# A mixture-of-experts decoder block: down-projection rows loaded in pairs, up-projection columns taken in the matching order, and the overflow table moved into the expert loop

## The chip, the cores and the metric

The kernel runs on one core of a Trainium2 chip. The metric is the device time of one execution in microseconds (us); several executions are timed and their median is given. Beside them one execution is taken with the hardware profiler, and every row below is from that one. TensorE multiplies matrices (its results go to PSUM), VectorE and ScalarE do the elementwise work, GpSimd issues the scattered writes, and SyncE's queue (SP) issues the weight loads, which 16 DMA engines carry out.

## The reference

One decoder block on 512 tokens of width 1024, all in float32: adaLN-modulated RMS norms, a gated linear recurrence (HGRN2) beside sliding-window attention, a merge, and then a mixture of 32 experts of which each token takes 4. The change is in the last part:

```
logits = h @ w_router + b_router;  gates = softmax(top 4 of logits)
per expert e, on the tokens that chose it:
    hu    = x @ w_up[e] + b_up[e]                 # 1024 -> 2048
    x_glu = min(hu[:, ::2], 7);  x_lin = clip(hu[:, 1::2], -7, 7)
    act   = x_glu * sigmoid(1.702 * x_glu) * (x_lin + 1)
    y     = act @ w_down[e] + b_down[e]           # 1024 -> 1024
out = x + g2 * sum over a token's experts of gate * y
```

Even columns of `w_up` make the gated half and odd columns the linear half.

## The kernel before, in words

Matrices are multiplied in fp16 with three products: each float32 weight tile of 128 partitions by 2048 floats is split into a high part (ScalarE, L341: `hi = fp16(w*2048)`) and a low part (VectorE, L346: `lo = fp16(w*2048 - hi)`), and TensorE adds hi*hi, hi*lo and lo*hi. The function `split` does this for all stages. It takes a loaded tile from a ring of 8 KB-per-partition buffers (named slot, slotb, slotc) and a second buffer of the same ring for the two fp16 halves. A staging buffer comes free when the low part is made, a split buffer when the matmuls that read it are done, and with each buffer that comes free `pump` issues the next load of a fixed list on SP's queue.

Each expert has 8 up tiles (128 rows of `w_up`, 2048 columns: one run of 8192 bytes per partition) and 4 down tiles (256 rows of `w_down`: two rows of 4096 bytes per partition, 128 rows apart). The first 3 down tiles are split, the last one goes to TensorE as float32. In the up split the even and odd columns are parted: `view_in` reads the tile as "all even columns, then all odd columns", a step of 2 floats within a partition, and the halves are written without a step. So row p of hidden block f of `act` is the hidden unit 128 f + p, which is what the down tile has in partition p.

The loop over experts is software-pipelined: for expert e come 8 steps of `up_k` (48 matmuls each), with the gather of the next expert's tokens between them (`pick`, L1150, copied by ScalarE at L1157), then `swiglu` (L1199 to L1216, VectorE and ScalarE in turn), then the down projection of expert e-1 (`down_j`), and its output rows scaled by `finish` (L1253) and added to DRAM by an indirect DMA (L1245). `up_bias` (L1183) puts the bias into the up banks. Splits run ahead of the matmuls: `ahead(i)` makes all splits up to LOOK = 6 tiles past tile i. Ahead of `swiglu` a further call, with `lows`, makes the high part of one more tile at once and its low part only after `swiglu`.

An expert's 96 token slots can overflow. `overflow_table` works out on VectorE how many further blocks there are, and a loop of that many trips runs after all experts; with these inputs it made none. The table is computed in the last trip of the expert loop, before the last down projection. The instructions of each engine run in the order in which the program issues them (L1388 to L1396 fix it).

L635 and the reductions L506, L993 and L1282, which the prediction uses as measures, are elsewhere: L635 multiplies columns 2s-1, 4s-1, ... of a tile by columns s-1, 3s-1, ... in place, for s = 1, 2, 4, ..., with 512/s elements a partition; L993 sums over 4 runs that lie 32 floats apart; L506 and L1282 sum over contiguous runs. L851 and L960 are plain multiplications and additions without a step, L1004 a plain ScalarE copy.

Of the kernel before, what the change touches and what calls it, by code (L numbers as in the profile page):

```python
# [41 lines left out]
def block_body(tc, x, c, positions, w_ada, b_ada, norm1_gain, w_in, lower_bound_logits, hg_norm_gain,  # L42
# [19 lines left out]
    with top:  # L62
# [41 lines left out]
        def dview(ap, off, dims):  # L104
            return bass.AP(tensor=ap.tensor, offset=ap.offset + off, ap=dims)
# [55 lines left out]
        def q_dn(e, j):  # L161
            queue(("dn", e, j), lambda t: SP.dma_start(
                t.rearrange("p (k f) -> p k f", k=2),
                dview(w_down, (e * 1024 + 256 * j) * 1024, [[1024, 128], [128 * 1024, 2], [1, 1024]])))
# [876 lines left out]
        def bias_up():  # L1041
            st = ready.pop(("bup",))
            src = st[:32, :].rearrange("p (f g) -> p g f", g=2)
            bk = sd_bank()
            for m in range(16):
                T.transpose(bk[:, 32 * m:32 * m + 32], src[:, m // 8, 128 * (m % 8):128 * (m % 8) + 128],
                            ident[:32, :32])
            A.activation(bu.rearrange("p e m -> p m e"), bk.rearrange("p (m e) -> p m e", m=16), AF.Copy, scale=SU)
            free(st)
# [7 lines left out]
        def split_up(e, k, later=None):  # L1057
            split(("up", e, k), 2048, later=later, view_in=lambda t: t.rearrange("p (f g) -> p g f", g=2),
                  view_hi=lambda t: t.rearrange("p (g f) -> p g f", g=2))
# [126 lines left out]
        def up_k(hl, k, xg):  # L1186
            for f in range(16):
                o = pu[f // 4][:, C * (f % 4):C * (f % 4) + C]
                for n, (pa_, pw) in enumerate(PASSES):
                    T.matmul(o, lhsT=hl[:, 2048 * pw + 128 * f:2048 * pw + 128 * f + 128], rhs=xg[:, pa_, k, :],  # L1190
                             start=False, stop=(k == KT - 1 and n == 2), skip_group_check=True)
# [65 lines left out]

        def overflow_table():
# [17 lines left out]
            V.tensor_copy(nblk[:, 0:1], cum[:, NE - 1:NE])  # L1276
            slot = hl_take()[0]
# [4 lines left out]
            V.tensor_reduce(eix, cmpt, axis=AX.X, op=OP.add)  # L1282
            eixi = moe.tile([128, NB], I32, name="eixi")
# [4 lines left out]
            V.tensor_sub(cum, cum, nbk)  # L1288
            V.tensor_tensor(cmpt, iota_e[:, None, :].to_broadcast([128, NB, NE]),
# [6 lines left out]
            return nblk, eix, eixi, beg  # L1296
# [39 lines left out]

        i = 0
        for e in range(NEX + 1):
            if e < NEX:
                prep = nexts.pop(e + 1, iter(()))  # L1340
                xg = state[e][0]
                for k in range(8):
# [4 lines left out]
                    hl_done(("up", e, k))  # L1347
                    i += 1
# [8 lines left out]
                ahead(i, lows)  # L1357
# [9 lines left out]
            if e == NEX:  # L1367
                tables = overflow_table()
# [32 lines left out]
        with tc.For_i(0, nreg, 1) as it:  # L1401
# [27 lines left out]
            for k in range(8):  # L1429
                stt = free_slots[0]  # L1430
                free_slots.rotate(-1)
                SP.dma_start(stt, wup[ds(er, 1)].rearrange("o k f -> (o k) f")[128 * k:128 * k + 128, :])
                slot, hl = hl_take()
                src = stt.rearrange("p (f g) -> p g f", g=2)
                hi, lo = (hl[:, :2048].rearrange("p (g f) -> p g f", g=2),
                          hl[:, 2048:].rearrange("p (g f) -> p g f", g=2))
                A.activation(hi, src, AF.Copy, scale=SW)
                V.scalar_tensor_tensor(lo, src, SW, hi, op0=OP.mult, op1=OP.subtract)
                up_k(hl, k, xg)
                hl_give(slot)  # L1440
# [4 lines left out]
            for j in range(4):  # L1445
# [3 lines left out]
                             wdn[ds(er, 1)].rearrange("o (j k p) f -> p (o j) k f", j=4, k=2)[:, j])  # L1449
# [16 lines left out]
LOOK = 6  # L1466
NHX = 6
# [27 lines left out]
```

## Time and profile before

| | before |
|---|---|
| median of 3 runs | 1500.58 us (1500.37 to 1503.2) |
| profiled execution | 1501.85 us, span 1500.1 us |
| mean granted TensorE clock | 0.986 of full |
| TensorE matmul busy | 1402.3 us (93% of the span) |
| VectorE busy | 1299.1 us (87%) |
| ScalarE busy | 1053.5 us (70%) |
| GpSimd busy | 358.4 us (24%) |
| moved by DMA | 476.44 MB, mean 318 GB/s |

The span is from the first to the last instruction; the time of the execution has a little around it. Busy time counts instructions that run, not those that wait. Matmuls are pipelined, so the mean duration of one is longer than the step from one to the next. A "step" of an operand in the texts is the distance between successive elements that an instruction reads within a partition.

### The profile page before, as it was taken

The numbers are of one execution on the slowest core, as the hardware profiler recorded it, in microseconds if no ns is written. First come the engines' busy times: TensorE is split into PE (matmuls) and PEld (weight loads), VectorE is DVE, ScalarE is ACT, GpSimd is POOL, SyncE is SP. The second block draws the span as 40 slices with busy tenths as digits, with TensorE's granted clock in tenths as the row PEclk, the third lists the DMA queues.
The fourth block names the chain that finished last, engine by engine and source line by source line (L and its number), as shares of the span: only waits on it lengthen the run. The fifth ranks groups of instructions, "written<-read, shape, count | busy, mean of one in ns | idle before, by whom it ended". The sixth has DMA issues, their size and how long they took to land. (4 is left out here: it accounts for less than half of the span.)

```text
span 1500.1 us, 41126 instructions
## 1 busy us (share of the span) xinstructions
PE 1402.3 (93%) x18200; PEld 1035.1 (69%) x18200; DVE 1299.1 (87%) x1457; ACT 1053.5 (70%) x1024; POOL 358.4 (24%) x82
## 2 busy tenths in 40 slices
PE   3979999999977999999999999999999999999994
PEld 2536567444557887788877888777887777888771
DVE  6876677777898999999999999999998899999885
ACT  4555424622548888888888888888887888888770
POOL 1020000010110233312433344203344333344400
PEclk9999999999989999999999999999999999999997
DMA  9832321376758999999999999999999999999971
GB/s 314 266 97 85 113 56 57 130 251 239 289 213 312 372 397 404 406 403 402 410 396 408 409 404 410 387 403 396 397 408 385 402 384 407 390 397 408 386 291 18
DMA packets 113521, 476.44 MB, mean 318 GB/s; under 512 B 10718, under 2 KB 35387, under 8 KB 80539
## 3 DMA queue, kind: packets, MB, share of 16 engines
q1 hardware_dynamic: 106160, 458.78, 77.8%
q0 software_dynamic: 5440, 12.72, 3.9%
q8 instruction: 144, 2.36, 0.6%
q10 hardware_dynamic: 1738, 2.27, 0.4%
q14 instruction: 39, 0.31, 0.1%
HBM read 463.22 MB, written 14.70 MB: 319 GB/s over the span
## 5 line engine op out<-in xcount | busy, mean ns | idle before, releaser
L1245 POOL DMA_INDIRECT out_dram<-y,idx x32 | 325.1, 10159 | 725.0 <-DVE y L1253 685.1
L1190 PE MATMUL pu<-xg,slot 128*128 128x96 f16 x10224 | 463.2, 206 | 10.5 <-issue 7.0
L1190 PEld LDWEIGHTS <-slot 128*128 128x128 f16 x10224 | 446.0, 98 | 28.6 <-issue 23.7
L346 DVE SCALAR_TENSOR_TENSOR slot<-slot,slot 128x2048 f16<-128x2048 f32 (+1 forms) x120 | 271.4, 2271 | 37.2 <-ACT slot L341 36.9
L341 ACT ACTIVATE slot<-slot 128x2048 f16<-128x2048 f32 (+1 forms) x120 | 242.2, 2031 | 79.1 <-DVE slot L346 24.6
L346 DVE SCALAR_TENSOR_TENSOR slot<-slotb,slot 128x2048 f16<-128x2048 f32 x101 | 227.7, 2282 | 8.2 <-ACT slot L341 7.9
L346 DVE SCALAR_TENSOR_TENSOR slot<-slotc,slot 128x2048 f16<-128x2048 f32 x97 | 219.7, 2283 | 12.6 <-ACT slot L341 12.4
L341 ACT ACTIVATE slot<-slotc 128x2048 f16<-128x2048 f32 x97 | 201.5, 2104 | 31.4 <-DMA slotc<-in_w_up_dram 9.9
L1241 PEld LDWEIGHTS <-act 128*96 128x96 f16 x1152 | 140.4, 124 | 115.5 <-issue 16.0
L341 ACT ACTIVATE slot<-slotb 128x2048 f16<-128x2048 f32 x101 | 197.4, 1957 | 32.0 <-PE pu L1190 11.4
L1241 PE MATMUL pd<-slot,act 128*96 128x512 f16 x924 | 206.4, 380 | 0.0
L701 PE MATMUL mm<-hT,slot 128*128 128x512 f16 x672 | 151.4, 381 | 0.0
L701 PEld LDWEIGHTS <-slot 128*128 128x128 f16 x672 | 65.5, 98 | 77.8 <-issue 2.9
L1150 PE MATMUL gb<-sel,h 128*128 128x96 f16 x1984 | 106.3, 208 | 11.7 <-ACT xg L1157 8.0
L1150 PEld LDWEIGHTS <-h 128*128 128x128 f16 x1984 | 92.4, 98 | 12.4 <-issue 10.3
L1190 PE MATMUL pu<-xg,slotb 128*128 128x96 f16 x2064 | 95.8, 206 | 4.2 <-issue 2.3
L1190 PEld LDWEIGHTS <-slotb 128*128 128x128 f16 x2064 | 90.7, 98 | 8.1 <-issue 7.1
L785 POOL DMA_DIRECT2D mdram<-mr x8 | 4.7, 591 | 270.0 <-DVE mr L779 207.0
L1233 PE MATMUL pd<-slot,act 128*96 128x512 f32 x144 | 64.7, 592 | 0.0
L1157 ACT ACTIVATE xg<-gb 128x384 f16<-128x384 f32 x124 | 59.1, 477 | 1.6 <-PE gb L1150 1.4
L1183 ACT ACTIVATE pu<-bu 128x384 f32<-128x384 f32 x128 | 57.0, 477 | 0.0
L346 DVE SCALAR_TENSOR_TENSOR slotb<-slot,slotb 128x2048 f16<-128x2048 f32 x20 | 45.8, 2289 | 11.6 <-ACT slotb L341 11.5
(339 smaller groups left out, 1634.9 us busy)
## 6 DMA issues: line engine op xcount, KB each, us to landing
slotc<-in_w_up_dram SPq DMA_DIRECT2D x116, 1024.0 KB, 19.4
slot<-in_w_up_dram SPq DMA_DIRECT2D x110, 1024.0 KB, 18.1
slotb<-in_w_down_dram SPq DMA_DIRECT2D x98, 1024.0 KB, 21.6
slotb<-in_w_up_dram SPq DMA_DIRECT2D x30, 1024.0 KB, 16.7
slot<-in_w_down_dram SPq DMA_DIRECT2D x20, 1024.0 KB, 22.5
slot<-in_w_in_dram SPq DMA_DIRECT2D x16, 1024.0 KB, 5.3
slot<-in_w_ada_dram SPq DMA_DIRECT2D x16, 1024.0 KB, 5.4
slotc<-in_w_down_dram SPq DMA_DIRECT2D x10, 1024.0 KB
```

The costliest lines, as they stand in the source:

```text
L341: A.activation(hi, src, AF.Copy, scale=SW)
L346: V.scalar_tensor_tensor(lo, src, SW, hi, op0=OP.mult, op1=OP.subtract)
L701: T.matmul(bk, lhsT=hl[:, o:o + 128], rhs=hT[:, ph, k, :], start=(k == 0 and n == 0), stop=(k == KT - 1 and n == 2))
L785: G.dma_start(mdram[q:q + 1, 512 * u:512 * u + 512], m)
L1150: T.matmul(bk[:, C * k:C * k + C], lhsT=h2[:, part, t, 128 * kk:128 * kk + 128], rhs=sel[:, t, :], start=(k == 0 and t == 0), stop=(t == N ...
L1157: A.activation(xg[:, part, 4 * u:4 * u + 4, :].rearrange("p k c -> p (k c)"), bk[:, :4 * C], AF.Copy)
L1183: A.activation(pu[i][:, :4 * C].rearrange("p (m c) -> p m c", m=4), b[:, 4 * i:4 * i + 4, None].to_broadcast([128, 4, C]), AF.Copy)
L1190: T.matmul(o, lhsT=hl[:, 2048 * pw + 128 * f:2048 * pw + 128 * f + 128], rhs=xg[:, pa_, k, :], start=False, stop=(k == KT - 1 and n == 2), ...
L1233: T.matmul(pd[u][:C, :], lhsT=act32[:, k - 4, :], rhs=w[:, o:o + 512], start=False, stop=(k == KT - 1))
L1241: T.matmul(pd[u][:C, :], lhsT=act[:, pa_, k, :], rhs=w[:, c0:c0 + 512], start=False, stop=False)
L1245: G.indirect_dma_start(out=out2, out_offset=bass.IndirectOffsetOnAxis(ap=idx[:n, :1], axis=0), in_=y[:n, :], in_offset=None, bounds_check= ...
```

## The change

A down tile now holds rows 2p and 2p+1 of its 256 rows in partition p, so that each partition gets one run of 8192 bytes. For `act` to lie in the same order, the up tile is read as four runs (columns 4f, 4f+1, 4f+2, 4f+3), each with a step of 4 floats in place of 2, and `up_k` and `bias_up` take the blocks of 128 columns in the order that this makes. The overflow loop after the experts is changed alike. `overflow_table` becomes a generator with three parts, which run in the up steps (k = 3) of experts 6, 8 and 10 and take and give back a buffer each. The look-ahead split before `swiglu` is left out at experts 0 and 31.

```diff
--- before.py
+++ after.py
@@ -160,8 +160,7 @@
 
         def q_dn(e, j):
             queue(("dn", e, j), lambda t: SP.dma_start(
-                t.rearrange("p (k f) -> p k f", k=2),
-                dview(w_down, (e * 1024 + 256 * j) * 1024, [[1024, 128], [128 * 1024, 2], [1, 1024]])))
+                t, dview(w_down, (e * 1024 + 256 * j) * 1024, [[2048, 128], [1, 2048]])))
 
         for g in range(4):
             q_ada1(g, 0)
@@ -1040,11 +1039,11 @@
 
         def bias_up():
             st = ready.pop(("bup",))
-            src = st[:32, :].rearrange("p (f g) -> p g f", g=2)
+            src = st[:32, :].rearrange("p (f r) -> p r f", r=4)
             bk = sd_bank()
             for m in range(16):
-                T.transpose(bk[:, 32 * m:32 * m + 32], src[:, m // 8, 128 * (m % 8):128 * (m % 8) + 128],
-                            ident[:32, :32])
+                k = m % 8
+                T.transpose(bk[:, 32 * m:32 * m + 32], src[:, 2 * (k % 2) + m // 8, 128 * (k // 2):128 * (k // 2) + 128], ident[:32, :32])
             A.activation(bu.rearrange("p e m -> p m e"), bk.rearrange("p (m e) -> p m e", m=16), AF.Copy, scale=SU)
             free(st)
 
@@ -1055,8 +1054,8 @@
             free(st)
 
         def split_up(e, k, later=None):
-            split(("up", e, k), 2048, later=later, view_in=lambda t: t.rearrange("p (f g) -> p g f", g=2),
-                  view_hi=lambda t: t.rearrange("p (g f) -> p g f", g=2))
+            split(("up", e, k), 2048, later=later, view_in=lambda t: t.rearrange("p (f r) -> p r f", r=4),
+                  view_hi=lambda t: t.rearrange("p (r f) -> p r f", r=4))
 
         order = []
         for e in range(NEX + 1):
@@ -1185,9 +1184,10 @@
 
         def up_k(hl, k, xg):
             for f in range(16):
+                cb = 512 * (2 * (f % 2) + f // 8) + 128 * (f % 8 // 2)
                 o = pu[f // 4][:, C * (f % 4):C * (f % 4) + C]
                 for n, (pa_, pw) in enumerate(PASSES):
-                    T.matmul(o, lhsT=hl[:, 2048 * pw + 128 * f:2048 * pw + 128 * f + 128], rhs=xg[:, pa_, k, :],
+                    T.matmul(o, lhsT=hl[:, 2048 * pw + cb:2048 * pw + cb + 128], rhs=xg[:, pa_, k, :],
                              start=False, stop=(k == KT - 1 and n == 2), skip_group_check=True)
 
         def swiglu(act, act32, read=None):
@@ -1255,6 +1255,8 @@
 
         NB = 32
 
+        tables = []
+
         def overflow_table():
 
             cb = pse.tile([128, 512], F32, name="gb", bufs=2)
@@ -1274,18 +1276,23 @@
             V.tensor_tensor_scan(cum, one_e, nbk, 0.0, op0=OP.mult, op1=OP.add)
             nblk = moe.tile([128, 2], I32, name="nblk")
             V.tensor_copy(nblk[:, 0:1], cum[:, NE - 1:NE])
+            yield
             slot = hl_take()[0]
             cmpt = slot[:, :NB * NE].rearrange("p (b e) -> p b e", b=NB)
             V.tensor_tensor(cmpt, iota_c[:, :NB, None].to_broadcast([128, NB, NE]),
                             cum[:, None, :].to_broadcast([128, NB, NE]), op=OP.is_gt)
             eix = moe.tile([128, NB], F32, name="eix")
             V.tensor_reduce(eix, cmpt, axis=AX.X, op=OP.add)
+            hl_give(slot)
             eixi = moe.tile([128, NB], I32, name="eixi")
             V.tensor_scalar(eix, eix, float(NE - 1), None, op0=OP.min)
             V.tensor_copy(eixi, eix)
             beg = moe.tile([128, NB], F32, name="beg")
 
             V.tensor_sub(cum, cum, nbk)
+            yield
+            slot = hl_take()[0]
+            cmpt = slot[:, :NB * NE].rearrange("p (b e) -> p b e", b=NB)
             V.tensor_tensor(cmpt, iota_e[:, None, :].to_broadcast([128, NB, NE]),
                             eix[:, :, None].to_broadcast([128, NB, NE]), op=OP.is_equal)
             V.tensor_mul(cmpt, cmpt, cum[:, None, :].to_broadcast([128, NB, NE]))
@@ -1293,7 +1300,8 @@
             V.tensor_sub(beg, iota_c[:, :NB], beg)
             V.tensor_scalar(beg, beg, float(C), None, op0=OP.mult)
             hl_give(slot)
-            return nblk, eix, eixi, beg
+            tables.extend((nblk, eix, eixi, beg))
+            yield
 
         def aux_of(e):
             return lambda t: aux[:, t, e, :]
@@ -1334,6 +1342,7 @@
                         next(prep, None)
                 up_bias(bu[:, 1], b)
 
+        table = overflow_table()
         i = 0
         for e in range(NEX + 1):
             if e < NEX:
@@ -1345,6 +1354,8 @@
                         next(prep, None)
                     up_k(hlmap[("up", e, k)], k, xg)
                     hl_done(("up", e, k))
+                    if k == 3 and e in TABLE_AT:
+                        next(table)
                     i += 1
                     if e == 0 and k == 4:
                         for t in range(NT):
@@ -1354,7 +1365,8 @@
                         hl_give(sel0slot)
                         A.activation(gate[:, 3:4], bu[:, 0, 0:1], AF.Silu)
                 lows = []
-                ahead(i, lows)
+                if 0 < e < NEX - 1:
+                    ahead(i, lows)
                 acts[e] = new_act()
                 swiglu(*acts[e], read=rest if e == 0 else None)
                 for low in lows:
@@ -1364,8 +1376,6 @@
                 if e + 2 < NEX:
                     nexts[e + 2] = prepare(e + 2)
                     next(nexts[e + 2])
-            if e == NEX:
-                tables = overflow_table()
             if e > 0:
                 _, gate, idx = state.pop(e - 1)
                 down_bias(E64[:, e - 1:e])
@@ -1431,9 +1441,9 @@
                 free_slots.rotate(-1)
                 SP.dma_start(stt, wup[ds(er, 1)].rearrange("o k f -> (o k) f")[128 * k:128 * k + 128, :])
                 slot, hl = hl_take()
-                src = stt.rearrange("p (f g) -> p g f", g=2)
-                hi, lo = (hl[:, :2048].rearrange("p (g f) -> p g f", g=2),
-                          hl[:, 2048:].rearrange("p (g f) -> p g f", g=2))
+                src = stt.rearrange("p (f r) -> p r f", r=4)
+                hi, lo = (hl[:, :2048].rearrange("p (r f) -> p r f", r=4),
+                          hl[:, 2048:].rearrange("p (r f) -> p r f", r=4))
                 A.activation(hi, src, AF.Copy, scale=SW)
                 V.scalar_tensor_tensor(lo, src, SW, hi, op0=OP.mult, op1=OP.subtract)
                 up_k(hl, k, xg)
@@ -1446,7 +1456,7 @@
                 stt = free_slots[0]
                 free_slots.rotate(-1)
                 SP.dma_start(stt.rearrange("p (k f) -> p k f", k=2),
-                             wdn[ds(er, 1)].rearrange("o (j k p) f -> p (o j) k f", j=4, k=2)[:, j])
+                             wdn[ds(er, 1)].rearrange("o (j p k) f -> p (o j) k f", j=4, k=2)[:, j])
                 if j >= 3:
                     down_j(stt, j, act, act32)
                     continue
@@ -1464,6 +1474,7 @@
 _OUTS = [((1, 512, 1024), 'float32')]
 NSB, NSC = 5, 4
 LOOK = 6
+TABLE_AT = (6, 8, 10)
 NHX = 6
 SW_AT = {0: 1, 1: 2, 2: 2, 5: 4, 6: 3, 7: 3, 8: 3, 9: 3, 10: 3, 11: 3, 12: 3, 13: 3}
 HG_AT = {9: 1, 10: 1, 11: 1, 12: 1, 13: 1, 14: 1, 15: 1, 16: 1, 17: 1}
```

## Rows read from the trace of the kernel before

**Rows 1.** The page, part 1: busy us of each engine, share of the span, instructions:

```profile
PE 1402.3 (93%) x18200; PEld 1035.1 (69%) x18200; DVE 1299.1 (87%) x1457; ACT 1053.5 (70%) x1024; POOL 358.4 (24%) x82
```

**Rows 2.** The SwiGLU clamp L1199 from 490 us on, and the timeline at 1429 us:

```profile
L1199 DVE TENSOR_SCALAR sg_g<-pu x62: 545/549/553, 500.5 to 1464.8; 128x384 f32<-128x384 f32 x62
...
1429.37 1.01 DVE L1199 TENSOR_SCALAR sg_g<-pu 128x384 f32<-128x384 f32 x2
```

**Rows 3.** The windows view: busy us (instructions), granted clock, DMA share, GB/s:

```profile
500.55:1429.37 928.82, 912.56 (x14466) 733.77 (x14464) 875.41 (x726) 781.91 (x667) 320.83 (x29) 1.00 1.01 399
```

**Rows 4.** The waits from 600 to 1400 us: us in total, times, longest:

```profile
DVE slot L346 <- ACT slot L341: 33.2, 57, 2.8
...
ACT act L1213 <- DVE sg_l L1210: 20.8, 25, 0.9
```

**Rows 5.** Lines L341 and L346 from 600 to 1400 us: duration min/median/max ns:

```profile
L341 ACT ACTIVATE slot<-slotb x82: 1910/1912/2126, 598.7 to 1385.2; 128x2048 f16<-128x2048 f32 x82
...
L341 ACT ACTIVATE slot<-slotc x74: 2047/2111/2168, 606.4 to 1376.7; 128x2048 f16<-128x2048 f32 x74
...
L346 DVE SCALAR_TENSOR_TENSOR slot<-slotb,slot x82: 2275/2280/2293, 601.1 to 1387.4; 128x2048 f16<-128x2048 f32 x82
...
L346 DVE SCALAR_TENSOR_TENSOR slot<-slotc,slot x75: 2272/2282/2294, 598.4 to 1380.8; 128x2048 f16<-128x2048 f32 x75
```

**Rows 6.** The page, part 6: DMA issues, KB each, us to landing:

```profile
slotc<-in_w_up_dram SPq DMA_DIRECT2D x116, 1024.0 KB, 19.4
...
slotb<-in_w_down_dram SPq DMA_DIRECT2D x98, 1024.0 KB, 21.6
```

**Rows 7.** Groups of instructions by shape, VectorE: busy us, mean ns | idle before:

```profile
L635 DVE TENSOR_TENSOR hf<-hf 128x512 f32<-128x512 f32 x2 | 1.4, 688 | 0.0
...
L635 DVE TENSOR_TENSOR hf<-hf 128x256 f32<-128x256 f32 x2 | 1.2, 624 | 0.0
...
L635 DVE TENSOR_TENSOR hf<-hf 128x128 f32<-128x128 f32 x2 | 0.8, 388 | 0.0
...
L851 DVE TENSOR_TENSOR sig<-sig 128x512 f32<-128x512 f32 x8 | 5.5, 686 | 0.2
...
L960 DVE TENSOR_TENSOR x<-x,xa 128x256 f32<-128x256 f32 x2 | 0.8, 414 | 0.0
```

**Rows 8.** The same view, VectorE's reductions:

```profile
L993 DVE TENSOR_REDUCE Mb<-oh 128x32 bf16<-128x128 f32 x4 | 1.5, 365 | 0.0
...
L506 DVE TENSOR_REDUCE qst<-qtmp 128x10 f32<-128x640 f32 x4 | 3.3, 820 | 1.9 <-ACT qtmp L505 1.9
...
L1282 DVE TENSOR_REDUCE eix<-slotb 128x32 f32<-128x1024 f32 x1 | 1.2, 1220 | 0.0
```

**Rows 9.** The same view, ScalarE:

```profile
L1004 ACT ACTIVATE h<-xa 128x1024 f16<-128x1024 f32 x3 | 3.2, 1054 | 4.9 <-DVE xa L1003 4.9
```

**Rows 10.** The windows view ahead of the loop, then of L346 alone (busy, count):

```profile
434.73:500.55 65.82, 51.49 (x1008) 47.66 (x1009) 57.93 (x89) 52.13 (x57) 0.57 (x1) 0.90 0.90 346
...
434.73:500.55 65.82, 40.43 (x18) 0.90 0.90 346
```

**Rows 11.** The timeline of the tail: start, us, instruction, idle before it:

```profile
1457.71 1.91 ACT L341 ACTIVATE slotb<-slot 128x2048 f16<-128x2048 f32 x1 [4.93 <-DMA slot<-in_w_down_dram]
...
1471.10 1.24 PE L1225 MATMUL pd<-bd,E 64*96 64x512 f16 x2 [7.37 <-DVE y L1253]
...
1471.63 0.17 DVE L1264 COPY cnt<-gb 128x32 f32<-128x32 f32 x1
...
1480.23 0.18 DVE L1294 TENSOR_SCALAR beg<-beg 128x32 f32<-128x32 f32 x1
...
1482.53 3.60 PE L1233 MATMUL pd<-slotc,act 128*96 128x512 f32 x8
```

**Rows 12.** The windows view in two stretches of little TensorE work:

```profile
435.00:440.00 5.00, 2.04 (x13) 1.00 (x13) 4.50 (x22) 3.31 (x7) 0.57 (x1) 0.62 1.01 426
...
470.00:475.00 5.00, 1.84 (x24) 1.84 (x24) 5.00 (x6) 3.85 (x5) 0.00 (x0) 0.53 0.94 339
```

## The prediction

> **What bounds the kernel now.** I read the engine totals first [rows 1]. TensorE, the DMA and VectorE are all near full, so no total says which one sets the pace, and the stage has to be cut out. The expert loop is the bulk of the run: the SwiGLU clamp of an expert (L1199, two per expert) opens expert 1's at 500.5 us and expert 30's at 1429.37 us [rows 2]. That is 29 experts in 928.8 us, or 32.03 us each. The window view of exactly that stretch [rows 3] gives the busy time per expert, each figure divided by 29: TensorE 31.47, VectorE 30.19, ScalarE 26.96 us, with the 16 DMA engines booked at 1.01 and 399 GB/s. So the loop is bound by DMA and TensorE together. VectorE has 1.84 us of air per expert, ScalarE 5.1. The wait view [rows 4] says the same of the coupling: over 25 experts VectorE waited 33.2 us for ScalarE's half of a weight split, some 1.3 us each in the group shown, and ScalarE 20.8 us for VectorE in the SwiGLU. Hardly anything can be gained here, and VectorE is the engine to which little can be added.
>
> What fills those two engines are the weight splits: 8 up tiles and 3 down tiles per expert, each one ScalarE copy (L341) and one VectorE subtraction (L346) of 128x2048. Their durations [rows 5], with the issue table [rows 6] to tell which staging buffers hold which weights (slotc nearly all up, slotb mostly down), are: ScalarE 1.91 us on down tiles (contiguous reading) and 2.11 on up tiles (every second float, a step of 8 bytes); VectorE 2.28 on both.
>
> **Part 1, the up columns in the new order: a step of 16 bytes.** The old up view reads its tile as 2 runs with a step of 2 floats; the new one reads 4 runs of 512 with a step of 4 floats, 16 bytes. Same instructions, same count (256 on each engine), same contiguous fp16 output; only the step of the source changes. No large instruction in the trace has that step, so I price it from the nearest rows.
>
> VectorE: L635 of the HGRN scan is one multiplication whose operands step by 2s floats with 512/s elements [rows 7]. At a step of 2 floats, 512 elements take 688 ns, which is what the contiguous L851 takes (686). At 4 floats, 256 elements take 624 ns, against 414 for the contiguous L960; at 8 floats, 128 take 388. The slope beyond 4 floats is (624-388)/128 = 1.84 ns per element; contiguous it is (686-414)/256 = 1.06. So a step of 2 is free and a step of 4 costs 0.78 ns more per element. On 2048 elements that is 1.60 us: 2.28 becomes 3.88. In L635 both inputs and the output step; in L346 one input does. For one stepping input alone there is the reduction L993 [rows 8]: 128 elements at a step of 32 floats take 365 ns. Contiguous reductions (640 in 820, 1024 in 1220) give 1.04 per element and hence 287 for 128. That is +0.61 per element, or +1.25 us on a tile. Bounds for VectorE: nothing, if only stepping outputs cost, to +1.60. The reduction excludes nothing clearly (its runs are only 4 long) but stands against zero.
>
> ScalarE: 1024 contiguous elements take 1.054 us [rows 9], 2048 take 1.911, so 0.20 is fixed. On up tiles 2.11-0.20 over 1024 pairs is 1.87 ns per 16 bytes touched. That is VectorE's 1.84 again: each engine seems to get one 16-byte piece per some 1.85 ns. Contiguous that feeds 4 floats and at a step of 2 two floats, which covers VectorE's 1.06 ns per float but not ScalarE's 0.84. At a step of 4 it feeds one. That two engines give one number is why I take the upper end for both: ScalarE 0.20+2048*1.87 = 4.03 us, +1.92. Lower bound for ScalarE: another 0.20, as from a step of 1 to 2.
>
> The Trainium skill has a rule for this: SBUF — State Buffer, in the note on cachelines under "Door 1: The DMA port swizzle", says that SBUF lines hold 16 bytes, that a line wants two hits for full rate, and that each access on a new line pays. It gives no price; by it the sum goes the way of the rows. The same note ends by calling a stride of up to 4 fp32 free; by that clause this part would cost nothing, and the time of rival (b) would come out. The step-4 row of VectorE contradicts that clause.
>
> **The new period.** Per expert VectorE gets 30.19+8*1.60 = 43.0 us and ScalarE 26.96+8*1.92 = 42.3, against 31.5 for TensorE and about as much for DMA. The bound moves to VectorE, with ScalarE hard behind, and the two alternate within each split (the subtraction needs the copy). Today's 1.3 us of VectorE waiting per expert stays, since the SwiGLU exchange and the four gather copies hit ScalarE at other moments than VectorE. I take 1.4: a period of 44.4 us, 12.4 more. Times 29: +359 us.
>
> Before the loop: from 434.73 to 500.55 us VectorE is busy 57.9 of 65.8 us [rows 10] and makes 18 subtractions, all of up tiles but expert 0's 3 down tiles. 15*1.60 = 24 us, less a part of the 7.9 us of air: +20. Three earlier copies lie beside other work of ScalarE and cost nothing here; uncovered they would cost 5.
>
> **Part 2, the down loads in 8192-byte packets.** The number of DMAs (128 down loads, issued from SP's queue, not moved past any other) and their bytes stay; 256 packets of 4096 bytes become 128 of 8192 each. The gain cannot exceed what TensorE leaves, 32.03-31.47 = 0.56 us per expert or 16 us in 29, nor fall below nothing. With a period of 44.4 the loads wait for compute, and it is worth nothing; alone it would sit in the 0 to 16. The down tiles' splits stay contiguous; the down matmuls take the same 1024-column halves.
>
> **Part 3, the overflow table and the two removed look-aheads.** The table ran in the tail, from 1471.63 to 1480.41 us on VectorE [rows 11], while TensorE did the last expert's down projection, whose last group of matmuls ends at 1486.13; there it cost nothing, so taking it away saves nothing. In the loop its 8.8 us land on the engine that then sets the pace: +9. With the old balance, VectorE's 1.84 us of air per expert would hide most of it. Not splitting ahead of expert 31's SwiGLU takes ScalarE copies that wait for DMA (4.93 us the longest) out of the way of that SwiGLU, and so the 7.37 us for which TensorE waits for y at 1471. I count -7 for it. But of the 256 up tiles 3, 15 and 29*8 are counted above, and the 6 left come after expert 30's SwiGLU: 6*1.60 = 9.6. Together +2. Not doing so at expert 0 only reorders within full engines: nothing; with its cover gone, one copy of 4 us. The 16 transposes of the up bias at a wider step are under 1 us.
>
> **Sum,** against the profiled execution's 1501.85 us (span 1500.1 and 1.75 around it; 1.27 above the median of the runs, 1500.58): 1501.85+359+20+9+2 = 1892 us; against the median that is 1.27 less, and I take 1890.
>
> **Rivals.**
> (a) A stepping input alone costs less: +1.25 us on VectorE as in the reduction, ScalarE by the same measure or by its own. VectorE 40.2 per expert plus 1.3 is 41.5, ScalarE at most 42.3 plus its waits 43.5. Time 1501.85+29*(9.5 to 11.5)+13+9 = 1799 to 1857. For it: only the reduction isolates an input. Against: ScalarE's up row is also input alone and gives 1.87.
> (b) Reading at 16 bytes costs VectorE nothing (its L635 price being that of the stepping output) and ScalarE another 0.20. This ends on the other side. It decides below 1.84/8 = 0.23 us per tile of added VectorE time: up to there the loop keeps its period, and then the larger packets give up to 0.56 us per expert and the tail up to 7. Time 1501.85-16-7 = 1479 at best to no change, 1488 in the middle. Against: the reduction, and ScalarE's 0.20 already at 8 bytes. It is also the time by the last clause of the note in the Trainium skill.
> (c) TensorE's clock. In the new loop TensorE gets an up tile about every 4 us and needs 2, for some 30 us of each 44. The granted clock was 0.62 and 0.53 of full in two stretches in which TensorE worked 2.04 and 1.84 of 5 us [rows 12], that is partly at the 1.2 GHz level. With half of its work at that level TensorE would need 31.47*1.5 = 47.2 us and set the pace: 1501.85+29*15.2+31 = 1973; with a third, 42.0 us, it stays hidden. Time 1930 to 2050. Against: it starts from nearly full work in the down part, and slower matmuls fill the gaps.
> (d) A partial price, between (b) and (a), 1510 to 1780.
>
> **How the numbers follow.** The forecast's own case, 1857 to 1930, gets 0.56, since three rows agree on the price and the period can hardly lie under 43. (a) 0.18, (c) 0.10, (d) 0.09, (b) 0.07, of which 0.01 is no change. The range leaves out (b), nearly all of (d) and the upper half of (c): 1765 to 1965. A measurement tells about 0.2% from no change: faster 0.06, within it 0.01, slower 0.93.
>
> **What would show it.** Right: L341 on up tiles near 4.0 us and L346 near 3.9, down tiles still at 1.91 and 2.28; SwiGLU to SwiGLU 44 us; DMA share near 0.73 and ScalarE no longer waiting for DMA; TensorE busy 71%. If L346 is near 3.5, (a); if both stay within 0.2 of now, (b); if the up matmuls spread and the granted clock in the loop is well under 1, (c). The prediction is wrong if the engines read a step of 16 bytes at a rate that no row here shows, or overlap such reading with something else.

## The result and the profile after

The changed kernel takes 1900.92 us (median; 1898.42 to 1901.64) against 1500.62 for the kernel before, beside which it was timed: a ratio of 1.266 [1.2641, 1.2678], 400 us slower. The forecast was 1890 with a range of 1765 to 1965. The profiled execution took 1901.62 us, its span is 1899.7.

The page of the changed kernel: engine totals, DMA line and issues (the totals answer to [rows 1], the issues to [rows 6]):

```profile
PE 1522.7 (80%) x18200; PEld 1146.1 (60%) x18200; DVE 1699.5 (89%) x1457; ACT 1500.0 (79%) x1024; POOL 565.3 (30%) x82
...
DMA packets 97136, 476.44 MB, mean 251 GB/s; under 512 B 10717, under 2 KB 35386, under 8 KB 47770
...
slotc<-in_w_up_dram SPq DMA_DIRECT2D x116, 1024.0 KB, 6.0
...
slotb<-in_w_down_dram SPq DMA_DIRECT2D x98, 1024.0 KB, 7.1
```

The counts are those of before; VectorE works 400 us longer (1299.1 to 1699.5) and ScalarE 447. The large packets did arrive; the same line of the kernel before is

```profile
DMA packets 113521, 476.44 MB, mean 318 GB/s; under 512 B 10718, under 2 KB 35387, under 8 KB 80539
```

But they are no longer what anything waits for: an up load lands 6.0 us after its issue where it took 19.4 [rows 6].

Lines 340 and 345 are the split (341 and 346 before); durations from 700 to 1800 us, minimum/median/maximum in ns, against [rows 5]:

```profile
L340 ACT ACTIVATE slot<-slotc x75: 3812/3947/4080, 703.1 to 1796.5; 128x2048 f16<-128x2048 f32 x75
...
L345 DVE SCALAR_TENSOR_TENSOR slot<-slotb,slot x80: 2255/2312/3937, 699.7 to 1766.3; 128x2048 f16<-128x2048 f32 x80
L345 DVE SCALAR_TENSOR_TENSOR slot<-slotc,slot x74: 3786/3870/3997, 708.2 to 1792.8; 128x2048 f16<-128x2048 f32 x74
```

Buffer slotc holds nearly only up tiles, and there both engines went from 2.11 and 2.28 us to 3.95 and 3.87. Buffer slotb holds mostly down tiles: its median stays at 2.31, its maximum is an up tile. So the step, not the kernel as a whole, carries the price.

The SwiGLU clamp L1199 (line of the same number before) divides the run into the same stretches as [rows 2]; the timeline of the changed kernel:

```profile
537.83 1.00 DVE L1199 TENSOR_SCALAR sg_g<-pu 128x384 f32<-128x384 f32 x2
...
581.37 1.03 DVE L1199 TENSOR_SCALAR sg_g<-pu 128x384 f32<-128x384 f32 x2
...
1819.96 1.01 DVE L1199 TENSOR_SCALAR sg_g<-pu 128x384 f32<-128x384 f32 x2
...
1862.64 1.02 DVE L1199 TENSOR_SCALAR sg_g<-pu 128x384 f32<-128x384 f32 x2
```

Expert 1's comes at 537.83 (500.55 before: +37.3). Experts 1 to 30 take 1282.1 us (928.8: +353.3). From expert 30's to the end of the span there are 79.7 us (70.7: +9.0). That is 399.6 of the 399.8 us between the two profiled executions.

The windows view of the changed kernel for the loop, as [rows 3], and for the stretch ahead of it, as [rows 10], each followed back to the same instruction:

```profile
537.83:1819.96 1282.13, 1018.12 (x14449) 833.04 (x14448) 1246.43 (x745) 1185.85 (x667) 526.31 (x29) 0.89 0.81 292
...
442.57:537.83 95.26, 62.97 (x1037) 55.80 (x1038) 81.52 (x88) 80.48 (x57) 0.57 (x1) 0.80 0.66 246
```

In the loop VectorE works 97% and ScalarE 92% of the time, TensorE 79%, and DMA fell from 1.01 to 0.81. Before, TensorE and DMA were the full ones.

The waits of the changed kernel over the same 29 trips:

```profile
PE pu L1190 <- ACT pu L1182: 132.9, 55, 3.4
PE gb L1149 <- ACT xg L1156: 128.7, 36, 8.9
ACT sg_s L1207 <- DVE sg_g L1199: 47.9, 29, 1.9
...
DVE slot L345 <- ACT slot L340: 27.1, 29, 2.5
...
ACT slot L340 <- DVE beg L1299: 9.0, 1, 9.0
ACT slot L340 <- DVE eix L1285: 7.8, 1, 7.8
...
PE gb L1149 <- DVE cnt L1266: 2.5, 1, 2.5
```

TensorE waits for ScalarE, VectorE and ScalarE wait for each other, and no row of this view names a transfer. The last three rows are the overflow table's parts, of which more below.

### The profile page after: what moved, and what is told of

Same layout as the page of the kernel before. It is cut to its first block, busy times and chain, and to the rows that moved or that the text cites. A ratio compares the mean times of both kernels' runs of the same rounds, so it can differ in the third digit from the quotient of the medians.

```text
span 1899.7 us, 41098 instructions
## 1 busy us (share of the span) xinstructions
PE 1522.7 (80%) x18200; PEld 1146.1 (60%) x18200; DVE 1699.5 (89%) x1457; ACT 1500.0 (79%) x1024; POOL 565.3 (30%) x82
## 5 line engine op out<-in xcount | busy, mean ns | idle before, releaser
L1245 POOL DMA_INDIRECT out_dram<-y,idx x32 | 530.6, 16581 | 911.2 <-DVE y L1253 897.6
L1190 PE MATMUL pu<-xg,slot 128*128 128x96 f16 x10224 | 541.3, 221 | 117.9 <-ACT pu L1182 114.9
L1190 PEld LDWEIGHTS <-slot 128*128 128x128 f16 x10224 | 523.9, 107 | 139.7 <-issue 134.4
L345 DVE SCALAR_TENSOR_TENSOR slot<-slot,slot 128x2048 f16<-128x2048 f32 (+1 forms) x120 | 417.3, 3486 | 35.9 <-ACT slot L340 35.8
L340 ACT ACTIVATE slot<-slot 128x2048 f16<-128x2048 f32 (+1 forms) x120 | 410.3, 3441 | 49.5 <-DVE slot L345 25.3
L345 DVE SCALAR_TENSOR_TENSOR slot<-slotc,slot 128x2048 f16<-128x2048 f32 x97 | 372.0, 3858 | 12.8 <-ACT slot L340 11.6
L340 ACT ACTIVATE slot<-slotc 128x2048 f16<-128x2048 f32 x97 | 375.4, 3909 | 2.6 <-PE pu L1190 2.6
L340 ACT ACTIVATE slot<-slotb 128x2048 f16<-128x2048 f32 x101 | 242.1, 2426 | 17.5 <-DVE beg L1299 9.0
L700 PEld LDWEIGHTS <-slot 128*128 128x128 f16 x672 | 65.7, 98 | 77.9 <-issue 3.4
L340 ACT ACTIVATE slotb<-slotc 128x2048 f16<-128x2048 f32 x20 | 78.8, 3940 | 3.9 <-DVE slot L345 3.9
L345 DVE SCALAR_TENSOR_TENSOR slotb<-slotc,slotb 128x2048 f16<-128x2048 f32 x20 | 77.5, 3873 | 4.1 <-ACT slotb L340 4.1
```

What stands on the lines that cost most here:

```text
L700: T.matmul(bk, lhsT=hl[:, o:o + 128], rhs=hT[:, ph, k, :], start=(k == 0 and n == 0), stop=(k == KT - 1 and n == 2))
L1190: T.matmul(o, lhsT=hl[:, 2048 * pw + cb:2048 * pw + cb + 128], rhs=xg[:, pa_, k, :], start=False, stop=(k == KT - 1 and n == 2), skip_grou ...
L1245: G.indirect_dma_start(out=out2, out_offset=bass.IndirectOffsetOnAxis(ap=idx[:n, :1], axis=0), in_=y[:n, :], in_offset=None, bounds_check= ...
```

## The experiments

Two theories were set against each other in the main. By the first, each of the two splitting engines handles one 16-byte piece of its source in some 1.8 ns, whichever float of it is wanted. By the rivals, the engines share that service (both slow down when they work at once), or the price grows with distance, or only steps of whole pieces cost.

**The price by itself.** The kernel m1_steps holds only the instructions in question on loaded data, the copies and subtractions twice each; `step(t, s)` takes every s-th element (cut to the calls):

```python
A.activation(hi, step(src, s), AF.Copy, scale=SW)           # s = 1, 2, 3, 4, 8 floats
V.scalar_tensor_tensor(lo, step(src, s), SW, hi, op0=OP.mult, op1=OP.subtract)
A.activation(step(wide, s), src[:, :N], AF.Copy, scale=SW)  # fp16 output, s = 2, 4, 8; VectorE's subtraction likewise
T.matmul(pu[:, :96], lhsT=step(wide[:, 128 * (r % 8):], s, 128), rhs=hi[:, :96], start=True, stop=True)
```

> No block at all: x is copied to the output, and the instructions in question are run by themselves, twice each: copies and subtractions of 128x2048 with the float32 input at steps of 1, 2, 3, 4 and 8 floats, fp16 outputs at steps of 1, 2, 4 and 8, weight loads at steps of 1, 2, 4 and 8 fp16, and last copies and subtractions at step 4 at the same time on both engines. Theory of one 16-byte piece per 1.85 ns: ScalarE 1.91, 2.1, 3.0, 4.0, 4.0 us; VectorE 2.28, 2.28, 3.0, 3.9, 3.9 us; the same with both running. A rival in which the cost grows with the distance: step 8 slower than step 4. A rival in which only powers of two or whole multiples of 16 bytes cost: step 3 as cheap as step 2.

The timeline of m1_steps: lines 68 to 77 are ScalarE's copies at steps 1, 2, 3, 4 and 8 in pairs, then VectorE's subtractions in the same order, one of each pair shown:

```profile
24.61 1.91 ACT L69 ACTIVATE hi<-src 128x2048 f16<-128x2048 f32 x1
26.56 2.01 ACT L70 ACTIVATE hi<-src 128x2048 f16<-128x2048 f32 x1
...
30.65 2.90 ACT L72 ACTIVATE hi<-src 128x2048 f16<-128x2048 f32 x1
...
36.51 3.80 ACT L74 ACTIVATE hi<-src 128x2048 f16<-128x2048 f32 x1
...
44.18 3.86 ACT L76 ACTIVATE hi<-src 128x2048 f16<-128x2048 f32 x1
...
54.30 2.29 DVE L82 SCALAR_TENSOR_TENSOR lo<-src,hi 128x2048 f16<-128x2048 f32 x1
...
58.95 2.29 DVE L82 SCALAR_TENSOR_TENSOR lo<-src,hi 128x2048 f16<-128x2048 f32 x1
...
64.17 2.86 DVE L82 SCALAR_TENSOR_TENSOR lo<-src,hi 128x2048 f16<-128x2048 f32 x1
...
70.86 3.75 DVE L82 SCALAR_TENSOR_TENSOR lo<-src,hi 128x2048 f16<-128x2048 f32 x1
...
78.50 3.82 DVE L82 SCALAR_TENSOR_TENSOR lo<-src,hi 128x2048 f16<-128x2048 f32 x1
```

The groups of m1_steps by shape (busy us, mean ns): both engines reading at step 4 at the same time, and ScalarE's contiguous reading with a stepping fp16 output (L96 step 2, L98 step 4, L100 step 8):

```profile
L127 ACT ACTIVATE both<-src 128x2048 f16<-128x2048 f32 x6 | 23.1, 3842 | 0.4 <-DVE lo L125 0.3
L82 DVE SCALAR_TENSOR_TENSOR lo<-srcb,hi 128x2048 f16<-128x2048 f32 x6 | 22.7, 3786 | 0.2
...
L100 ACT ACTIVATE wide<-src 128x2048 f16<-128x2048 f32 x1 | 9.3, 9262 | 0.0
...
L98 ACT ACTIVATE wide<-src 128x2048 f16<-128x2048 f32 x1 | 4.7, 4742 | 0.0
...
L96 ACT ACTIVATE wide<-src 128x2048 f16<-128x2048 f32 x1 | 2.5, 2466 | 0.0
```

Step 3 is the telling row. Its 2048 elements lie in 1536 pieces, 4 elements in every 3; with step 4's price of (3.80-0.20)/2048 = 1.76 ns a piece and the prediction's 0.20 fixed that is 2.90 us, which is what was measured (VectorE 2.86). Step 8 costs hardly more than step 4 (3.86 against 3.80), so distance is not the cause. Together, reading two different tiles, the engines take 3.84 and 3.79 (3.80 and 3.75 alone), so they do not share the service. The three rivals fall, and with them the reduction's lower price for a stepping input, rival (a).

The weight loads of the same run matter below. With fp16 columns 2, 4 and 8 bytes apart one started about every 42.5 ns (106 loads of some 0.1 us ran in the 4.4 us from 157.6 us: 4.5/106), with columns 16 bytes apart every 60 ns (36 loads of 0.157 us in the 2 us from 163.6 us: 2.157/36).

**One engine at a time.** Two kernels made from the one before, with its column order, loads and table, in which the up tile is read at 16 bytes by one engine alone (the fp16 side then steps by 4 bytes):

```diff
+            def wide(q, src_=False):
+                if src_:
+                    return q.rearrange("p (f h g) -> p h g f", h=2, g=2)
+                return q.rearrange("p (g f h) -> p h g f", h=2, g=2)
-            A.activation(hi, src, AF.Copy, scale=SW)
+            A.activation(wide(hl[:, :n]), wide(st, True), AF.Copy, scale=SW)     # e3_act16, up tiles
-                V.scalar_tensor_tensor(lo, src, SW, hi, ...)
+                    V.scalar_tensor_tensor(wide(hl[:, 2048:2048 + n]), wide(st, True), SW, wide(hl[:, :n]), ...)  # e4_dve16, up tiles
```

> The kernel before, with ScalarE's copy of up tiles alone reading at a step of 16 bytes (and writing fp16 at a step of 4 bytes, so that the layout stays); VectorE's subtraction stays at 8 bytes. Theory (each engine by itself gets one 16-byte piece per 1.85 ns): the copy takes 3.9 us as in the changed kernel, ScalarE needs 26.96+8*1.83 = 41.6 us per expert and its waits 1 to 2, so the period is 42.5 to 43.5 and the time 1820 to 1860. Rival: the two engines share what serves them, and alone the copy takes about 3 us: period about 35 to 36, time 1590 to 1640.

> The kernel before, with VectorE's subtraction on up tiles alone reading its float32 input at a step of 16 bytes (its fp16 input and output at a step of 4 bytes); ScalarE's copy stays at 8 bytes. Theory: the subtraction takes 3.87 us as in the changed kernel, VectorE needs 30.19+8*1.59 = 42.9 us per expert, period 43 to 43.6, time 1830 to 1860. Rival, shared service: about 3 us alone, period 36, time about 1620.

ScalarE alone: 1803.81 us, 1.2015 [1.1993, 1.2037], a trip 41.30 us. VectorE alone: 1853.37 us, 1.2345 [1.2323, 1.2368], a trip 43.08 us. The windows view from 700 to 1700 us, and the copies of slotc from 600 to 1700 us (busy us, mean ns), first of e3_act16:

```profile
700.00:1700.00 1000.00, 819.94 (x12122) 671.43 (x12122) 740.73 (x602) 994.90 (x557) 34.18 (x24) 0.92 0.84 312
...
L346 ACT ACTIVATE slot<-slotc 128x2048 f16<-128x2048 f32 x82 | 321.6, 3958 | 0.0
```

and of e4_dve16, with its subtractions:

```profile
700.00:1700.00 1000.00, 806.37 (x11531) 653.88 (x11531) 996.29 (x585) 620.66 (x540) 436.14 (x23) 0.90 0.83 299
...
L351 DVE SCALAR_TENSOR_TENSOR slot<-slotc,slot 128x2048 f16<-128x2048 f32 x78 | 303.0, 3910 | 0.0
```

The copy alone takes 3.96 us and the subtraction alone 3.91, as both do together in the changed kernel; the fp16 side's step of 4 bytes added next to nothing. Each engine alone already sets the pace, at 99.5 and 99.6% busy, and the other has 26 to 38% of air. The losses don't add: 41.3 and 43.1 alone, 43.55 together. ScalarE's extra is nearly hidden behind VectorE's. For ScalarE alone I had expected a trip of 42.5 to 43.5 us and 1820 to 1860 in all, because of waits that it turned out not to have; 1803.81 is a miss.

**The step undone, all else kept.** The pairs, the large packets, the moved table and the removed look-aheads stay. In e1_pairs_step2 the engines read at step 2 and TensorE takes every second fp16 column of the weights, in e2_pairs_contig at step 1 and every fourth (shortened):

```diff
-view_in=lambda t: t.rearrange("p (f r) -> p r f", r=4), ...
+view_in=lambda t: t.rearrange("p (f g) -> p g f", g=2), ...          # e2: no view
-cb = 512 * (2 * (f % 2) + f // 8) + 128 * (f % 8 // 2)
+cb = 1024 * (f // 8) + 256 * (f % 8 // 2)                            # e2: 512 * (f % 8 // 2)
-lhsT=hl[:, 2048 * pw + cb:2048 * pw + cb + 128]
+lhsT=hl[:, 2048 * pw + cb:2048 * pw + cb + 256].rearrange("p (n r) -> p r n", r=2)[:, f % 2, :]
+lhsT=hl[:, 2048 * pw + cb:2048 * pw + cb + 512].rearrange("p (n r) -> p r n", r=4)[:, 2 * (f % 2) + f // 8, :]   # e2
```

> The changed kernel with its pairs of rows, 8192-byte packets, moved table and removed look-aheads, but the up split reads with the old step of 2 floats, and TensorE picks every second fp16 column of the split weights instead. My theory: the whole loss is the step of 16 bytes in the splits, so this comes out at 1480 to 1501 us, L341-type copies of up tiles back at 2.1 us and subtractions at 2.28, and TensorE's weight loads at a step of 4 bytes stay near 98 ns. Rival: the pairing of rows or the larger packets cost something themselves, then it stays above 1520. Second rival: TensorE pays for the stepped weights, then weight loads are well over 98 ns and the time is over 1550.

> The pairs, the 8192-byte packets, the moved table and the removed look-aheads all stay; ScalarE and VectorE split each up tile without any step, and TensorE picks every fourth fp16 column of the weights instead. If the whole loss is the 16-byte step on the two splitting engines, it is gone: the up copy at 1.91 us (the down tile's price) where it was 3.93 in the changed kernel, the SwiGLU period near 31.5 us, and a time of 1,485 to 1,493 us, at most a few us under the 1,492.57 of the version at step 2, because ScalarE saves 8 x 0.2 = 1.6 us an expert and is not the engine that ends last. If the order of the columns costs wherever it is read, TensorE's weight loads now pay for it: 384 loads an expert at the 60 ns that the loads 16 bytes apart took instead of 42.5 would be +6.7 us an expert and about 1,690 us. The loads 8 bytes apart were issued every 42.5 ns, so I expect the former.

e1: 1492.57 us, 0.9938 [0.9924, 0.9952]. e2: 1490.41 us, 0.9931 [0.9918, 0.9945]. All of the loss is gone in both. The groups of e2_pairs_contig by shape, from 700 to 1300 us:

```profile
L1189 PE MATMUL pu<-xg,slot 128*128 128x96 f16 x6000 | 272.3, 206 | 7.2 <-issue 7.1
L1189 PEld LDWEIGHTS <-slot 128*128 128x128 f16 x6000 | 263.4, 113 | 17.8 <-issue 17.5
...
L340 ACT ACTIVATE slot<-slotc 128x2048 f16<-128x2048 f32 x59 | 112.8, 1913 | 31.1 <-issue 22.4 <-PE pu L1189 6.5
...
L1148 PEld LDWEIGHTS <-h 128*128 128x128 f16 x1200 | 55.4, 98 | 5.3 <-issue 5.2
```

The new order costs no time when TensorE picks the columns, here 8 bytes apart: its loads take 113 ns instead of the 98 of the contiguous L1148, but the up matmuls keep a mean of 206 ns. ScalarE's copies fall to 1.91, which the time can't tell from e1's 2.1: the intervals lie over one another.

**Which part made these two faster than before.** e5_part3 is the kernel before with the table in trips 6, 8 and 10 and without the two look-aheads; e9_pairs_alone is e1 with the table in the tail and all look-aheads, which is this difference to e1 (shortened):

```diff
-                    if k == 3 and e in TABLE_AT:
-                        next(table)
-                if 0 < e < NEX - 1:
-                    ahead(i, lows)
+                ahead(i, lows)
+            if e == NEX:
+                for _ in table:
+                    pass
```

> The kernel before with the overflow table moved into trips 6, 8 and 10 and the two look-aheads removed, and nothing of the pairs. If the packets are what made the version at step 2 faster by 9 us, this one stays near 1,500 (1,497 to 1,503). If the moved table and the missing look-ahead gave it, this one comes to 1,492 as well. The table's three parts cost that version 35.28 - 31.65 = 3.6 and 36.59 - 31.65 = 4.9 us in two trips, and take some 9 us out of the tail, so they should come out about even: I expect 1,497 to 1,502.

> The pairs and the 8192-byte packets alone, with the up split at step 2 as before: the table stands in the tail and all look-aheads are back. If the packets are worth the 9 us, this one is at 1,490 to 1,494; if the table and the look-aheads were, it is at 1,499 to 1,502. I expect 1,492, with the SwiGLU period at 31.65 us in every trip (32.03 before) because transfers land sooner, and the first SwiGLU 3 us sooner.

The pairs alone: 1492.75 us, 0.9934 [0.9922, 0.9947]. The table and the look-aheads alone: 1499.17 us, 0.9988 [0.9977, 0.9999], at most a quarter of a percent. So the 8192-byte packets are worth about 9 us once the read stays short. What of it comes from fewer packets and what from the order in which they arrive was not tried. I had expected expert 0's SwiGLU 3 us sooner in e9; it came at 473.3 us as before (473.6), and the gain is in the loop, 31.78 us a trip instead of 32.03.

**The moved table.** In the changed kernel the trips that end at the SwiGLU of experts 6, 8 and 10, whose up steps carry the table, took 47.90, 50.17 and 51.38 us, all others some 43.55. That is 18.8 us more, where the prediction had 9. The timeline at the second part, both engines:

```profile
827.70 1.89 ACT L340 ACTIVATE slotb<-slotb 128x2048 f16<-128x2048 f32 x1
837.35 1.91 ACT L340 ACTIVATE slot<-slotb 128x2048 f16<-128x2048 f32 x1 [7.76 <-DVE eix L1285]
...
834.68 1.25 DVE L1282 TENSOR_TENSOR slot<-iota_c,cum 128x1024 f32<-128x1024 f32 x1
835.96 1.22 DVE L1285 TENSOR_REDUCE eix<-slot 128x32 f32<-128x1024 f32 x1
...
839.29 4.49 DVE L345 SCALAR_TENSOR_TENSOR slot<-slotb,slot 128x2048 f16<-128x2048 f32 x2 [1.58 <-ACT slot L340]
845.64 3.88 DVE L345 SCALAR_TENSOR_TENSOR slot<-slot,slot 128x2048 f16<-128x2048 f32 x1 [1.86 <-ACT slot L340]
```

The table's comparisons are written into one of the six rotating buffers of the split weights. ScalarE's next copy needs it and stands idle for 7.76 us, first until VectorE has finished the subtractions that come ahead of the table's part, then until its reduction has read the buffer; after that VectorE waits for copies. Two kernels ask about it: e6_table_tail puts the table back (the first and the last hunk above), e10_table_buffer leaves it in the trips and gives it memory of its own:

```diff
-            slot = hl_take()[0]
-            cmpt = slot[:, :NB * NE].rearrange("p (b e) -> p b e", b=NB)
+            cmpt = own.rearrange("p (b e) -> p b e", b=NB)      # own: [128, NB * NE], allocated once
...
-            hl_give(slot)
```

> The changed kernel with only the overflow table put back into the tail. The three trips that carry its parts took 4.35, 6.6 and 7.8 us longer than the others, 18.8 us together, and the tail would take back about 9 us. If the table's parts sit on the path that two equally loaded engines set, the time falls by 10 us, to 1,891. If they only filled slack, or the transfers' delay after them is made up in later trips, it rises by 9, to 1,910. I expect 1,888 to 1,894.

> The changed kernel, the table still in trips 6, 8 and 10, but its comparisons are written into a buffer of their own instead of one of the six rotating buffers of the split weights. VectorE's busy time over the 29 trips was 8.86 us longer with the table in them than without, the time 18.8 us, and ScalarE waited 9.0 and 7.8 us for the table's buffer. If that wait is the other half, ScalarE can copy on through the table's parts and only VectorE's work is added: the trips with the table 1 to 4 us longer than the others instead of 4.35, 6.6 and 7.8, some 9 to 11 us in all, and the time near 1,892. If the two engines lose it because each copy is followed by a subtraction and neither gets ahead, the buffer makes no difference and the time stays at 1,898 to 1,902. I expect 1,892.

e6: 1880.5 us, 1.2526 [1.2504, 1.2547] to the kernel before. The fall is 20 us and not the 10 that I expected: back in the tail the table costs nothing, as the prediction had said; 36.1 us lie behind expert 31's SwiGLU with the table there, 37.1 in the changed kernel and 36.0 and 36.1 in e10 and e11, which have it in the loop. The windows view of e6 over its 29 trips:

```profile
537.21:1800.55 1263.34, 1019.20 (x14443) 834.79 (x14442) 1237.57 (x726) 1185.29 (x667) 548.37 (x29) 0.89 0.82 296
```

VectorE works 8.86 us less there than in the changed kernel, but the stretch is 18.8 us shorter: the other 9.9 were VectorE's idle time. e10: 1893.02 us, 1.262 [1.2595, 1.2645]. This interval just touches that of the changed kernel, so the trips have to carry it: 47.75, 46.39 and 47.56 us, 11.0 over the others instead of 18.8, the two parts that use the buffer giving 7.6 of it back. The second part's trip in e10, from expert 7's SwiGLU to expert 8's (50.17 us in the changed kernel):

```profile
803.75 1.02 DVE L1199 TENSOR_SCALAR sg_g<-pu 128x384 f32<-128x384 f32 x2
...
850.14 1.02 DVE L1199 TENSOR_SCALAR sg_g<-pu 128x384 f32<-128x384 f32 x2
```

The first part, which uses no such buffer, keeps its 4.2 us with 1.8 us of VectorE work. Its count stands in a PSUM bank that the gather uses too, and the trace of the changed kernel shows the gather's matmul, and with it ScalarE, waiting for VectorE to copy it out (PE gb <- DVE cnt, 2.5 us). No run took that away, so that it makes the rest of the 4.2 us is not shown.

**The three early copies.** Expert 0's first three up tiles are split in the logits stage. e11_early3 reads these three contiguously and lets TensorE pick every fourth column:

```diff
+            if e == 0 and k < 3:
+                split(("up", e, k), 2048, later=later)
+                return
```

> The changed kernel with expert 0's first three up tiles, those split at 387 to 405 us in the logits stage, read without a step (TensorE picks every fourth column of these three). Everything else stays at 16 bytes. The prediction gave these copies no cost, since ScalarE has other work beside them; the trace of the changed kernel shows that stage 7.8 us longer. If they are on a chain there (copy, subtraction, the next copy), the stage gives 7 to 8 us back and the time is 1,893. If the 7.8 us came from elsewhere, the time stays at 1,900.

1892.04 us, 1.2612 [1.2587, 1.2637]: 8.9 us less, and expert 1's SwiGLU at 529.18 instead of 537.83. Its timeline at expert 1's SwiGLU:

```profile
529.18 1.01 DVE L1204 TENSOR_SCALAR sg_g<-pu 128x384 f32<-128x384 f32 x2
```

The timeline of the changed kernel shows the chain that it cut:

```profile
397.26 3.89 ACT L340 ACTIVATE slot<-slot 128x2048 f16<-128x2048 f32 x1 [0.58 <-DVE slot L345]
...
401.19 3.83 DVE L345 SCALAR_TENSOR_TENSOR slot<-slot,slot 128x2048 f16<-128x2048 f32 x1 [1.58 <-ACT slot L340]
...
405.05 3.92 ACT L340 ACTIVATE slot<-slot 128x2048 f16<-128x2048 f32 x1 [3.90 <-DVE slot L345]
...
409.00 3.77 DVE L345 SCALAR_TENSOR_TENSOR slot<-slot,slot 128x2048 f16<-128x2048 f32 x1 [1.87 <-ACT slot L340]
```

Copy, subtraction and the next copy follow one another without overlap, so the tiles here pay both engines' increase.

**A candidate for the best.** e8_contig_table_tail is e2 with the table back in the tail.

> The version with the pairs and contiguous splits, and the overflow table back in the tail, as a candidate for the best of all. Its trips with the table were 35.28 and 35.94 us against some 31.5 for the others, less the short trips behind them (30.08) some 5 us. If the table in the tail is hidden, as it is in the changed kernel without it (the stretch behind expert 31's SwiGLU 36.1 us against 37.1), the time falls by 4 to 5 us to 1,485 to 1,487. If a loop at 0.99 of the DMA engines' time gets its transfers back after each such trip, it stays at 1,490. I expect 1,487.

1490.7 us, 0.9933 [0.9918, 0.9947]: not faster than e2, and not the 1,487 that I expected. Of the two ways that I had put down the second is what came. It fits that the DMA engines stay full there (booked at 1.01 over the loop of e2), and that in e2 short trips (30.08 us) follow the long ones of the table; no run asks about it further. e1, e2, e8 and e9 all beat both kernels, the one before by 0.5 to 0.8%, and can't be told apart.

## Why the prediction was right, point by point

- **What bounds, and what would bound then: right.** VectorE became the full engine with ScalarE next to it, and TensorE and DMA got air. Two of the signs were off: in the loop TensorE was busy 79% of the time instead of 71, and the DMA share was 0.81 instead of 0.73, although the bytes per second fell as forecast (292 of 399 GB/s are 0.73). TensorE's longer work goes with its clock, see the last point; why the DMA engines were booked longer for the same bytes stays open.
- **The price of the step: right.** Predicted 3.88 us for VectorE and 4.03 for ScalarE on an up tile, measured 3.87 and 3.95; the down tiles were unchanged. VectorE's price came from L635, in which the output steps too; that the input alone costs as much is what m1_steps added. The inference from two engines' numbers to one piece per 1.85 ns is borne out by it within 5% (1.76). On the Trainium skill: the note on cachelines under "Door 1: The DMA port swizzle" on the page SBUF — State Buffer wants two hits on each 16-byte line, and the trace of m1_steps agrees with that: at a step of 2 floats, two of a line, 2.01 us instead of 1.91 on ScalarE and 2.29 as before on VectorE. The clause that a stride of up to 4 fp32 is free does not hold here (1.91 us became 3.80 on ScalarE, 2.29 became 3.75 on VectorE).
- **The period: right, a little high.** 44.4 us predicted, 43.55 measured in the trips without table. VectorE's work is 1237.57/29 = 42.67 us (predicted 43.0), its idle time 0.89 (taken 1.4). The prediction kept the waits of before; fuller engines left fewer. 29 trips: +334 instead of +359.
- **The table in the loop: right in sign, too small.** 18.8 instead of 9, since the prediction counted VectorE's work (8.86) and not the buffer that the work holds (7.6).
- **Before the loop: too small by 17.** +37.3 instead of +20. VectorE's extra work in the stretch of [rows 10] was 23.6 us, as worked out (24). But its idle time there grew from 7.9 to 13.7 us where the prediction let it shrink, and the three early copies, costed at nothing (or 5 uncovered), took 7.8 with their subtractions (e11_early3 gives 8.7 back).
- **The tail: +9 instead of +2.** From expert 30's SwiGLU to 31's it took 42.68 us instead of 34.99; the stretch with the six dear up tiles grew by 7.7, where 9.6 were predicted for them. The -7 for the removed look-ahead did not come: TensorE's wait for y went from 7.37 [rows 11] to 4.45 us, but behind expert 31's SwiGLU 1.3 us were added (0.3 to 0.4 in e6, e10 and e11, which have the removal too). In the old balance its worth isn't settled either: from expert 30's SwiGLU to the end e1 has 67.4 us against 69.7 in e9, but e5 has 71.4 against 70.7 in the kernel before.
- **Sum.** 37.3+353.3+9.0 = 399.6 against 390 predicted. The period made the loop 25 us too high; the start, the table and the tail were 34 too low. That the total is off by only 10 us is luck in part: the period alone was off by 25 and the start by 17.
- **Part 2, the packets: right as far as it was tried.** Alone they gave about 9 us, within the 0 to 16 that were given. That they are worth nothing at the new period is argued from the waits, which name no transfer; no run took them out of the changed kernel.
- **Rival (c), TensorE's clock.** In the loop the granted clock was 0.89 of full (1.00 before), partly at the 1.2 GHz level, and TensorE's work in a trip grew from 31.47 to 1018.12/29 = 35.1 us. That stays under 43.6 us: the mechanism is there and hidden, as the prediction's "with a third it stays hidden" said.

## What to carry to other kernels

Before two full engines are made to read in a new order, ask which engine can take the order for nothing: here TensorE's weight loads picked every fourth column, 8 bytes apart, without cost to the time, while the same order on VectorE and ScalarE cost 400 us. (At 16 bytes apart the loads were slower, 60 ns instead of 42.5 in m1_steps.) Price a step by the 16-byte pieces that it touches as well as by its elements, and take the larger; at 4 fp32 every element is a piece. Work that is moved into a loop costs its time and also what it holds while others wait: 9 us of VectorE work cost 19, and 11 with a buffer of its own.

## What the runs showed of the hardware that was not expected

Stepping an fp16 output is dearer than stepping a float32 input, and grows with the step. In m1_steps fp16 outputs at 4, 8 and 16 bytes took ScalarE 2.47, 4.74 and 9.26 us for 128x2048, VectorE 2.53, 4.70 and 9.22, against 1.91 and 2.29 contiguous. Reading levels off at one piece per element; writing fp16 went on doubling up to the longest step tried, and why stays open. It is not so for every output: L635 of the kernel before writes float32 at steps of 16 and 32 bytes, and there an element costs 1.84 ns [rows 7], about the price of reading.
